# Reordering an eight-core hybrid decoder step on Trainium2: two tiles interleaved at the start, one output step moved, one factor kept in PSUM, later down-projections

## The chip, the cores and the metric

The kernel runs on all 8 NeuronCores of one Trainium2 chip, two dies of four cores (0 to 3 and 4 to 7). Every core works on its own sequence and its own 16 running tokens, so the cores don't exchange data, but they share the chip's memory. The metric is the device time in microseconds (us) of the slowest core. A few executions of any of these kernels fall in a slower state: some cores show a lower granted TensorE clock and the time is several per cent longer. All comparisons below are between fast executions.

## The reference, cut to what matters

One layer of a decoder trunk with 1024 channels: two token mixers in parallel (a causal pooling one and a gated short convolution), merged by sigmoid gates, then a gated feed-forward part with a short convolution. RMS norms stand before and after both parts.

```python
def trunk_layer(x, ...):
    h = rmsnorm(x, g_pre_mix)
    z = h @ w_in                                   # 1024 -> 4096
    u, v, bg, cg, ga, gb = jnp.split(z, IN_SPLITS, axis=-1)
    a, new_pool = multiscale_pool(u, buf_pool, pos0, w_pool, pool_scale)
    cv, new_conv = causal_dwconv(cg * v, buf_conv, w_conv)
    b = (bg * cv) @ w_conv_out
    merged = jax.nn.sigmoid(ga) * a + jax.nn.sigmoid(gb) * b
    x = x + rmsnorm(merged @ w_o, g_post_mix)
    h = rmsnorm(x, g_pre_ffn)
    upc, new_ffn = causal_dwconv(h @ w_up, buf_ffn, w_ffn_conv)    # 1024 -> 5632
    gate, val = jnp.split(upc, 2, axis=-1)
    y = (jax.nn.silu(gate) * val) @ w_down                         # 2816 -> 1024
    x = x + rmsnorm(y, g_post_ffn)
    return x, new_pool, new_conv, new_ffn
```

## The kernel before

Channels lie on the partitions and tokens along the free axis. One core's columns are cut into five mixing tiles (tile 0 of 512 columns, tiles 1 to 4 of 392) and then into six feed-forward (FFN) tiles of 344. The parts of a mixing tile, as the text calls them:

- **first half**: 16 blocks of the input projection (`F_block`), 8 matmuls each, with convolution and pooling on VectorE (DVE);
- **gates and merges** (`B`): 16 more blocks of the input projection for the gates, and 8 merges, which need the weights `w_pool` and `w_co`;
- **output step** (`WO`): 64 matmuls with `w_o`; ScalarE (ACT) evacuates each block into the buffer `R` and its square into `XSQ2`;
- **epilogue** (`epi`): the RMS factor, x added by an accumulating DMA, the result written to HBM by a DMA on the SyncE (SP) queue ("y write", in two halves), the second norm, and `h2` written to HBM for the FFN.

An RMS sum over the channels is made by DVE (`tree`, which adds 8 squares down to 2) and then two matmuls with a matrix of ones (`sums`), which go to a PSUM bank of their own. The other seven banks go round.

```python
def sums(rows, n, lo=0):
    pe([(bank(SB, n, lo), ONES, buf.ap[:, j, lo:n]) for buf, k, m in rows ...],
       ..., [("ps", SB)], n - lo, flt=True)        # flt: may float to another place in PE's order

def ln_exp(i, n, sq=None, lo=0):                   # rstd = exp(-0.5 * ln(mean + eps))
    s = SD.ap[:, i, lo:n]                          # in SBUF
    act(... out=s, in_=bank(SB, n, lo), func=AF.Ln ...)
    ...
    act(... out=s, in_=s, func=AF.Exp, scale=-0.5 ...)

def wo_evac(t, b, m):
    act(... out=R[t].ap[:, m, lo:N], in_=bank(b, N, lo), scale=cc(C_G2 + m) ...)       # L722
    act(... out=XSQ2[t].ap[:, m, lo:N], in_=bank(b, N, lo), func=AF.Square ...)        # L724

def epi_r(t, q):
    ...                                            # R *= rstd; R += x
    if q % 2:
        sp_dma(yT[:, ...], R[t].ap[...], [R[t].t(4 * h, 4)], [("y", t, h)], ...)       # the y write

def epi_x(t, k):
    if last:                                       # tile 4: scales R in place, so it needs the y write done
        act(... out=r, in_=r, scale=cc(C_G3 + k) ..., [..., ("y", t, k // 4)], ...)    # L776
        ...

def epi_y(t):                                      # end of an FFN tile
    sums([(YSQ, 0, 2)] ..., NB)
    ln_exp(0, NB)
    ...
    for q in range(4):                             # Y *= rstd, L868
        dve(... out=Y.ap[:, 2*q:2*q+2, :], in0=Y..., in1=SD.ap[:, 0, 0:NB]..., op=ALU.mult ...)
        pool_dma(yT[...], Y.ap[...], ..., acc=True)
```

A small scheduler in Python puts all operations into one order for each engine. PE's matmuls keep the order of the program, but the floating `sums` may go in where its model of time says that they are ready. Its rule for that is the line of the diff that begins with `if c is None or ready`, with `FLT` = 2500 ns. The cost model only decides the order; nothing in this document takes a time from it.

```python
    B(0)
    for t in range(1, NTA):                        # NTA = 5
        for i in range(16):
            F_block(t, i)
            if t == L: wup(1)                      # L = 4; one up-projection weight block is loaded
        if t < L:
            load_x(t + 1, 2, after=[wo[7]])
            ...
            prenorm(t + 1)
            WO(t - 1)
            epi(t - 1)
        ...
        B(t)                                       # for t == 4 with wup(2) after each merge
        if t == L - 1:
            WO(t, split=True)                      # tile 3's output step
            epi(t)
    WO(L, split=True, hook=lambda: wup(1))
    load_h2(0)                                     # the first FFN tile's input
```

`R` is one piece of memory for tiles 1 to 4. The weights of `w_in`, `w_co`, `w_up` and `w_dn` are read as f32 and cast to bf16 by DMAs on GpSimd's queue.

## Time and profile before

| | before |
|---|---|
| median of 3 runs | 844.45 us (842.34 to 845.41) |
| span of the slowest core in the profile (core 4) | 843.8 us |
| PE busy | 804.4 us |
| matmul work at full rate (5108 matmuls) | 792.0 us |

The last figure is an estimate. The Trainium skill, "TensorE: Matmul & The Clock Gate", Part 1 ("Wait — 56ns, not 53.3ns?"), gives N / 2.4 GHz + about 2.5 ns between the starts of warm back-to-back matmuls of N columns. The trace agrees: the median distances between the starts of two matmuls are 166 ns at 392 columns (the rule gives 165.8), 147 at 346 (146.7) and 216 at 512 (215.8). So what a matmul's distance to the next exceeds this rule is called *lost time* below. It contains waits and also matmuls at half the clock.

The page of the profile of the kernel before: busy time of the engines, and then PE's busy share and its granted clock in 40 equal slices of the span, in tenths.

```profile
PE 804.4 (95%) x5108; PEld 498.3 (59%) x5108; DVE 567.6 (67%) x1039; ACT 475.6 (56%) x924; POOL 261.5 (31%) x292
...
PE   6988899999999899999999999999999999999993
...
PEclk9997999999999999999999999999999999999997
```

TensorE is the bound: it is busy in nearly every slice, and no other engine comes over 67%. Only gaps can be won. They lie mainly in the first five slices, in slice 14 and in the last one. The windows view of core 4 before resolves four stretches. The columns are the window, its length, then busy us and instructions of PE, of PE's weight loads, of DVE, of ACT and of POOL, the granted clock, the DMA share and GB/s.

```profile
60.00:80.00 20.00, 14.93 (x55) 5.82 (x53) 6.30 (x10) 5.83 (x9) 5.00 (x7) 0.74 1.13 184
80.00:100.00 20.00, 17.50 (x82) 8.35 (x81) 12.77 (x21) 10.21 (x14) 0.00 (x0) 0.91 0.69 103
280.00:300.00 20.00, 17.71 (x98) 9.81 (x97) 10.56 (x19) 12.06 (x22) 1.46 (x2) 0.91 0.27 89
...
380.00:400.00 20.00, 20.00 (x138) 13.34 (x137) 18.60 (x37) 14.45 (x30) 19.95 (x18) 1.00 1.14 153
```

From 60 to 80 us PE ran 55 matmuls of 498 columns (210 ns each at full rate), or about 11.6 us of work; it shows as 14.93 us busy because part of them ran at half the clock. The waits view of PE in the kernel before says what it stood for (total us, times, the longest):

```profile
PE ps L463 <- DMA big<-w_co: 4.2, 2, 2.8
PE ps L463 <- ACT big L843: 3.4, 3, 1.2
...
PE ps L463 <- DMA big<-w_in: 3.2, 3, 2.3
...
PE ps L463 <- DVE big L544: 2.5, 1, 2.5
PE ps L463 <- ACT big L722: 2.3, 1, 2.3
```

`w_co` and `w_in` are the gate and merge weights of tile 0, which PE reaches before they have landed. L544 is tile 1's normalization. L722 is the evacuation of tile 3's output step; L843 is the evacuation of down-projections into `Y`. The timeline of core 4 before around 291 us shows what held L722 (start us, us, engine, line, operation, count, and in brackets the idle time before it and what ended it):

```profile
291.36 4.39 DVE L781 SCALAR_TENSOR_TENSOR big<-big 128x392 bf16<-128x392 f32 x8 [7.10 <-ACT big L724]
292.08 4.41 ACT L722 ACTIVATE big<-ps,big 128x392 f32<-128x392 f32 x8
...
292.81 5.49 PE L463 MATMUL ps<-big 128*128 128x392 bf16 x22 [2.29 <-ACT big L722]
```

DVE's L781 is the last step of tile 2's epilogue, which reads `R`; tile 3's evacuation follows it, and PE follows that, since its banks are full. The line view of the two multiplies by the RMS factor in the FFN of the kernel before (duration min/median/max in ns, first and last start in us, form):

```profile
L868 DVE TENSOR_TENSOR big<-big x20: 858/866/3450, 496.6 to 815.3; 128x688 f32<-128x688 f32 x20
```

```profile
L860 DVE TENSOR_TENSOR big<-big x4: 868/1588/2303, 832.2 to 836.0; 128x688 f32<-128x688 f32 x4
```

One of these multiplies takes 866 ns in the median and up to four times that.

### The profile page before, as it was taken

The page shows a single profiled execution, that of the slowest core. Times are in us where ns is not written, and L with a number is a line of the kernel's source. Part 1 is how long each engine was busy: PE and PEld are TensorE (multiplying, and loading weights), DVE is VectorE, ACT ScalarE, POOL GpSimd, SP SyncE. Part 2 cuts the span into 40 slices and gives each one's busy share as a digit, 9 for nine tenths or more (in the row PEclk, how much of TensorE's full clock was granted, in tenths as well). Part 3 has the DMA queues.
Part 4 walks back from the last instruction along what each step waited for, and adds up shares of the span by engine and source line. Part 5 has one row for each costly group of instructions (what it writes and reads, how often), then busy time and mean ns, then how long its engine had stood idle before and what let it go on. Part 6 is the DMA issues. An engine that isn't in the chain of part 4 may idle for free.

```text
span 843.8 us, 16663 instructions; the slowest of 8 cores (834.1 to 843.8 us)
## 1 busy us (share of the span) xinstructions
PE 804.4 (95%) x5108; PEld 498.3 (59%) x5108; DVE 567.6 (67%) x1039; ACT 475.6 (56%) x924; POOL 261.5 (31%) x292
## 2 busy tenths in 40 slices
PE   6988899999999899999999999999999999999993
PEld 4433455555555555566566666666666666666662
DVE  2753765787786587589776576568666865877723
ACT  3232569567656635787755555556555545665632
POOL 4532000201001063479582243224222422342222
PEclk9997999999999999999999999999999999999997
DMA  8999602813523499999990041014001500030062
GB/s 161 164 190 170 152 12 66 206 52 97 131 74 45 120 156 222 173 174 156 211 174 3 3 75 27 26 34 69 35 2 34 69 1 2 11 59 2 2 136 85
DMA packets 63206, 75.51 MB, mean 89 GB/s; under 512 B 2928, under 2 KB 59376, under 8 KB 63104
## 3 DMA queue, kind: packets, MB, share of 16 engines
q0 software_dynamic: 40720, 43.01, 35.6%
q1 hardware_dynamic: 22400, 31.45, 12.0%
q8 instruction: 43, 0.70, 0.3%
q14 instruction: 43, 0.35, 0.1%
HBM read 81.89 MB, written 22.90 MB: 124 GB/s over the span
## 4 chain that ended last, share of the span: by engine, by line
PE 84%; DMA 8%; issue 2%; DVE 2%; ACT 2%; POOL 1%; DVEq 0%; SPq 0%; ACTq 0%; POOLq 0%
PE ps L463 84%; DMA big<-w_co 4%; DMA big<-w_in 2%; DMA yT<-big 1%; DMA big<-xT 1%; POOL big L476 1%; DVE big L819 1%; ACT big L815 1%; DVE big L860 0%; ACT big L517 0%; DVE big L868 0%; ACT L517 0%; POOL big L755 0%; DVE big L544 0%; POOL big L833 0%
## 5 line engine op out<-in xcount | busy, mean ns | idle before, releaser
L463 PE MATMUL ps<-big 128*128 128x346 bf16 (+5 forms) x5108 | 804.4, 321 | 26.5 <-ACT big L532 4.8
L463 PEld LDWEIGHTS ps<-big 128*128 128x128 bf16 x5108 | 498.3, 99 | 332.2 <-issue 42.7
L819 DVE SCALAR_TENSOR_TENSOR big<-ps,big 128x344 f32<-128x344 f32 (+1 forms) x528 | 283.8, 570 | 95.9 <-ACT big L815 75.4
L833 POOL TENSOR_TENSOR big<-big 128x344 bf16<-128x344 f32 x132 | 125.6, 953 | 240.1 <-DVE big L819 172.0
L815 ACT ACTIVATE big<-ps,big 128x344 f32<-128x344 f32 (+1 forms) x264 | 140.0, 540 | 65.2 <-PE ps L463 61.5
L832 ACT ACTIVATE big<-big 128x344 f32<-128x344 f32 x132 | 64.1, 489 | 53.2 <-DVE big L819 50.8
L474 POOL DMA_DIRECT2D big<-xT x16 | 17.7, 1118 | 186.3 <-DVE big L705 108.4
L692 ACT ACTIVATE big<-ps 128x392 f32<-128x392 f32 (+1 forms) x80 | 38.9, 513 | 53.5 <-PE ps L463 28.5
L705 DVE SCALAR_TENSOR_TENSOR big<-ps,big 128x392 f32<-128x392 f32 (+1 forms) x40 | 25.8, 646 | 45.5 <-PE ps L463 41.4
L476 POOL DMA_DIRECT2D big<-w_up x36 | 29.1, 883 | 59.7 <-PE ps L463 52.3
L843 ACT ACTIVATE big<-ps,big 128x344 f32<-128x344 f32 x48 | 25.7, 546 | 36.4 <-PE ps L463 36.3
L507 DVE TENSOR_TENSOR big<-big 128x1568 bf16<-128x1568 bf16 (+3 forms) x28 | 22.7, 812 | 19.7 <-ACT big L724 19.1
L474 POOL DMA_DIRECT2D yT<-big x20 | 25.9, 1470 | 30.4 <-DVE big L819 16.0
L846 ACT ACTIVATE big<-ps 128x344 bf16<-128x344 f32 x48 | 21.7, 451 | 21.7 <-PE ps L463 18.3
L849 DVE TENSOR_TENSOR big<-big 128x688 bf16<-128x688 bf16 x17 | 8.8, 517 | 36.3 <-ACT big L846 36.3
L601 DVE TENSOR_TENSOR big<-big 128x406 f32<-128x406 f32 (+7 forms) x50 | 30.0, 600 | 3.6 <-ACT big L623 0.7
L868 DVE TENSOR_TENSOR big<-big 128x688 f32<-128x688 f32 x20 | 25.0, 1276 | 9.1 <-ACT big L522 9.1
L570 ACT ACTIVATE big<-big 128x392 f32<-128x392 f32 (+1 forms) x20 | 12.8, 639 | 31.7 <-DVE big L656 31.7
L722 ACT ACTIVATE big<-ps,big 128x392 f32<-128x392 f32 (+1 forms) x40 | 24.0, 608 | 10.2 <-PE ps L463 7.6
L476 POOL DMA_DIRECT2D big<-w_in x32 | 23.2, 745 | 19.9 <-DMA big<-xT 9.2
L573 DVE SCALAR_TENSOR_TENSOR big<-big 128x392 f32<-128x392 f32 (+1 forms) x40 | 25.6, 644 | 4.5 <-ACT big L570 3.8
L709 DVE TENSOR_TENSOR big<-ps,big 128x392 f32<-128x392 f32 (+1 forms) x40 | 23.4, 585 | 6.5 <-PE ps L463 5.7
(58 smaller groups left out, 379.9 us busy)
## 6 DMA issues: line engine op xcount, KB each, us to landing
big<-w_in POOLq DMA_DIRECT2D x32, 256.0 KB, 21.1
big<-w_up POOLq DMA_DIRECT2D x28, 256.0 KB, 21.0
yT<-big POOLq DMA_DIRECT2D x20, 344.0 KB, 5.5
yT<-big SPq DMA_DIRECT2D x8, 784.0 KB, 8.9
big<-w_dn POOLq DMA_DIRECT2D x8, 704.0 KB, 35.5
big<-xT SPq DMA_DIRECT2D x6, 784.0 KB, 4.8
big<-xT POOLq DMA_DIRECT2D x12, 392.0 KB, 7.2
big<-h2T SPq DMA_DIRECT2D x6, 692.0 KB, 4.6
```

The source lines that it names most:

```text
L463: ins = e.matmul(o, lhsT=l, rhs=x, start=(start and i == 0), stop=(stop and i == last))
L474: return S.add("pool", lambda e: e.dma_start(out=out, in_=in_, accum_op=ALU.add, max_dma_last_dim=mx), r, w, dma=True, byts=byts, pri=pri, ...
L476: return S.add("pool", lambda e: e.dma_start(out=out, in_=in_, max_dma_last_dim=mx), r, w, dma=True, byts=byts, pri=pri, after=after)
L573: dve(lambda e, k=k: e.scalar_tensor_tensor(out=cv, in0=p[:, 2 + k + lo:2 + k + N], scalar=cc(C_WC + 4 * k + c), in1=cv, op0=ALU.mult, op1 ...
L601: dve(lambda e, nx=nx, cur=cur, s=s, a2=a2: e.tensor_tensor(out=nx[:, a2:W], in0=cur[:, a2:W], in1=cur[:, a2 - s:W - s], op=ALU.add), [ct] ...
L692: act(lambda e, b=b, g=g: e.activation(out=GT[t].ap[:, g, lo:N], in_=bank(b, N, lo), func=AF.Sigmoid), [("ps", b)], [GT[t].t(g, 1)], N, ps ...
L705: dve(lambda e: e.scalar_tensor_tensor(out=A_, in0=bank(bp, N, lo), scalar=cc(C_PS + m), in1=A_, op0=ALU.mult, op1=ALU.mult), [("ps", bp), ...
L815: act(lambda e, b=b, fj=fj, tt=tt: e.activation(out=tt[:, 0:n], in_=bank(b, n), func=AF.Copy, scale=cc(C_WF + fj)), [("ps", b), KCST], [to ...
L819: dve(lambda e, b=b, fj=fj, tt=tt, k=k: e.scalar_tensor_tensor(out=tt[:, 0:n], in0=ps[:, b * 512 + k:b * 512 + k + n], scalar=cc(C_WF + 44 ...
L832: act(lambda e: e.activation(out=g, in_=g, func=AF.Silu), [T.t(0, 1)], [T.t(0, 1)], NB, tab="silu")
L833: S.add("pool", lambda e: e.tensor_tensor(out=gb.ap[:, j, :], in0=g, in1=v, op=ALU.mult), [T.t()], [gb.t(j, 1)], dur=NB * 2.17 + 100)
L843: act(lambda e: e.activation(out=Y.ap[:, m, :], in_=bank(b, NB), func=AF.Copy, scale=cc(C_G4 + m)), [("ps", b), KCST], [Y.t(m, 1)], NB, ps ...
```

## The change

Four things are moved, and no matmul is added or removed:

1. The first half of tile 1 is interleaved with the last blocks of tile 0's first half and goes before tile 0's gates and merges; tile 0's output step follows its merges. The gate weights get more time to land. Tile 1's x is loaded by GpSimd's queue between the weights, and the first weight loads wait for one quarter of tile 0's x instead of two. Buffers are laid out anew for it.
2. Tile 3's output step and epilogue move from before tile 4's first half to after seven of its blocks.
3. The FFN's RMS factor is kept in PSUM, so that the multiply has one SBUF input instead of two; and the eight down-projections of an FFN tile start at the sixth pair of up-projections instead of the third.
4. The rule for the floating sums is eased: a sum that the program needs soon may go in when it is modelled to be ready 400 ns ahead, instead of 2500 ns.

```diff
-                        if c is None or ready[f.idx] + FLT <= s or sf <= s - 200.0:
+                        if c is None or ready[f.idx] + (FLT if f.pri > s + 8000.0 else 400.0) <= s or sf <= s - 200.0:
...
-    X = per_tile(KC, False, [o_x] * NTA)
-    R = per_tile(KC, False, [o_r] + [X[1].end] * 4)
+    X = per_tile(KC, False, [o_x, W_O.off] + [o_x] * 3)
+    R = per_tile(KC, False, [o_r] + [X[2].end] * 4)
...   (other buffers of tile 1 moved in the same way)
-    def ln_exp(i, n, sq=None, lo=0):
+    def ln_exp(i, n, sq=None, lo=0, ps_out=False):
         s = SD.ap[:, i, lo:n]
+        out, tok = (bank(SB, n, lo), ("ps", SB)) if ps_out else (s, SD.t(i, 1))
...
-        ln_exp(0, NB)
+        ln_exp(0, NB, ps_out=True)
+        sdb = bank(SB, NB).unsqueeze(1).to_broadcast([128, 2, NB])
...   (both multiplies of epi_y read sdb)
-    wd += [wload(W_IN, w_in, i, 1, BL, after=[xs0[1]]) for i in range(1, 16)]
+    wd += [wload(W_IN, w_in, i, 1, BL, after=[xs0[0]]) for i in range(1, 16)]
...
+    for q in range(4):
+        pool_dma(X[1].flat[...], xT[1][...], ..., after=[xs0[1]], pri=-1e6)
...
-    for i in range(NRAW, 16):
+    prenorm(1)
+    wo = [wload(W_O, w_o, m, 1, BL, after=[xs0[1]]) for m in range(8)]
+    for i in range(NRAW, 12):
         F_block(0, i)
-    load_x(1, 4, after=[wd[20]])
-    prenorm(1)
+    for i in range(4):
+        F_block(1, i)
+        F_block(0, 12 + i)
+    for i in range(4, 16):
+        F_block(1, i)
...
     B(0)
+    load_x(2, 2, after=[wo[7]])
+    prenorm(2)
+    WO(0, split=True)
+    epi(0)
+    B(1)
+    load_states()
+    for t in range(2, L):
...   (as before for tiles 2 and 3)
+    for i in range(16):
+        F_block(L, i)
+        wup(1)
+        if i == 6:
+            WO(L - 1)
+            epi(L - 1)
+    small_states()
+    B(L)
...
-    WD = {2: 0, 5: 1, 8: 2, 10: 3, 13: 4, 15: 5, 18: 6, 21: 7}
+    WD = {5: 0, 7: 1, 10: 2, 12: 3, 14: 4, 16: 5, 19: 6, 21: 7}
```

A line of the kernel after has a number one higher than the same line before, from the end of `sums` on (L868 before is L869 after, L722 is L723).

## The prediction

> **What bounds the kernel now.** TensorE. The page shows it busy 804 of 843.8 us, and 84% of the chain that ended last is its matmuls. In the table of 20 us stretches PE is at 20.00 nearly everywhere, DVE at 11 to 19. So only PE's gaps can be won. From start-to-start distances of matmuls in the trace (slowest core; yardstick: about 123 matmuls of 392 columns in a steady 20 us) I estimate 792 us of matmul work and 36 us lost between first and last matmul:
> - 0 to 40 us: 8.5 us (x and first weights arrive).
> - 40 to 95 us: 15 us (other cores 7.5 to 14). Tile 0's gates and merges wait for weights: the waits view has PE <- DMA w_co 4.2 and w_in 3.2 us; the stretch 60:80 has PE busy 14.9 us at clock 0.74; 2.5 us are a wait for tile 1's normalization (L544). The Trainium skill, "TensorE: Matmul & The Clock Gate" (HAM oscillation), says idle gaps over about 3.4 us halve the clock[...].
> - 287 us: 4.1 us, ACT's evacuation of tile 3's output step (L722) waiting for DVE L781: tiles 2 and 3 share R.
> - 500, 580, 660 us: 1.3 us each, at the third pair of a tile. DVE's Y*rstd multiplies (L868) have a median of 866 ns but a maximum of 3450 ns.
> - the rest: about 4 us in 400-415 and at the last down-projections.
>
> **The change.** No matmul is added or removed.
> 1. Tile 1's first half (128 matmuls, 21 us) moves ahead of tile 0's merges and needs only weights already there. Gate weights then have until about 69 us instead of 46; they land by about 69 before, with the same bytes. The waits of 40-95 go: -14 us. Cost: tile 1's x (1.6 MB; its load took about 10 us beside the weights) cuts in after about four weight blocks and delays later ones by about 5 us; as weights start about 3 us earlier, I charge +2 us. DVE has about 50 us of work in 20-70 us; pooling can be put off into the merges.
> 2. Tile 3's output step after seven blocks of tile 4: epilogue 2 has long read R: -4 us.
> 3. rstd in PSUM: the multiply then has one SBUF input. The Trainium skill, "SBUF — State Buffer" (Who interferes with whom), says two SBUF inputs contend with a GpSimd op that reads SBUF, one doesn't; L868's 866 to 3450 ns agrees. I expect all near 870 ns. With the first down-projection three pairs later, the 1.3 us stalls go: -4 us; the tail (L860, 6.1 us for four) wins 0.5 to 1.
> 4. Earlier float-in of the sums, and tile 0's output step straight after its merges: perhaps +1 us.
>
> Sum: about -20 us, nearly all on the critical path. Predicted 824.5 us, range 817 to 833. Chances: faster by over 2% 0.70, within 2% 0.29, slower 0.01.
>
> **Would show it right.** PE at 20.00 and clock 1.00 in all stretches from 40 to 100 us; no PE <- DMA w_co; no stall near 270-290; L868 maximum under 1000 ns; PE <- ACT L843 gone.
>
> **Would make it wrong.** Weight blocks after x1 over 5 us late, so the loss moves to 25-40 us; DVE too full in 40-70 us, so evacuation holds the PSUM banks; sums floated in before their squares are ready; tile 3's epilogue colliding with up-projection loads; six pairs without down-projection overfilling DVE.

## The result, and the profile after

| | before | after |
|---|---|---|
| median | 844.93 us (842.34 to 846.17, 4 runs) | 832.31 us (831.09 to 832.64, 4 runs) |
| ratio of fast runs | | 0.9852, 95% interval 0.9826 to 0.9878 |
| span of the slowest core in the profile | 843.8 us | 830.5 us (core 5) |
| mean span of the 8 cores in the profile | 840.0 us | 827.8 us |

A ratio here is the mean time of one kernel's fast runs over that of the other's of the same rounds, so it is not quite the ratio of the medians. All runs were correct. The change gains 12.6 us, or 1.5%; it is faster, but by less than the 2% which the prediction thought most likely.

The lost time by phase, in us, as the mean of the eight cores (worked out from the starts of all matmuls in the traces; a gap counts where it begins; the first FFN tile runs from 3 us before the first up-projection to 62 us after it, and the last down-projections begin after the last up-projection, about 31.5 us before the last matmul):

| | to 40 us | 40 to 100 us | 100 us to FFN | first FFN tile | rest of FFN | last down-projections | after the last matmul | sum |
|---|---|---|---|---|---|---|---|---|
| before | 8.1 | 12.4 | 4.2 | 1.4 | 4.2 | 1.7 | 13.4 | 45.4 |
| after | 11.4 | 0.1 | 0.0 | 7.8 | 0.3 | 2.0 | 11.6 | 33.3 |
| gain | -3.3 | +12.3 | +4.2 | -6.4 | +3.8 | -0.3 | +1.8 | +12.1 |

The sum of gains, 12.1 us, accounts for the drop of the mean span (840.0 to 827.8 us). The new loss is in the first FFN tile. The windows view of core 5 after, with the columns as before:

```profile
20.00:40.00 20.00, 17.46 (x76) 7.62 (x75) 16.25 (x27) 7.78 (x14) 8.93 (x13) 0.91 1.12 203
...
60.00:80.00 20.00, 20.00 (x110) 10.66 (x109) 15.28 (x29) 7.62 (x18) 6.24 (x9) 1.00 1.15 159
80.00:100.00 20.00, 20.00 (x97) 9.33 (x96) 8.70 (x13) 5.49 (x10) 0.00 (x0) 1.00 0.82 171
280.00:300.00 20.00, 20.00 (x123) 11.81 (x121) 13.50 (x30) 11.18 (x22) 4.96 (x7) 1.00 0.92 135
340.00:360.00 20.00, 17.57 (x119) 11.20 (x117) 9.68 (x18) 13.45 (x25) 7.40 (x10) 1.00 1.09 156
380.00:400.00 20.00, 16.75 (x115) 10.97 (x113) 17.47 (x33) 15.26 (x31) 16.35 (x16) 1.00 1.15 200
```

The stretches 60 to 100 and 280 to 300 us are full now, at clock 1.00. A new gap stands at 20 to 40 us, and two more at 340 to 360 and 380 to 400, where the kernel before had 20.00 (at 380). The waits of PE in the kernel after (core 5):

```profile
PE ps L463 <- DVE big L507: 4.2, 2, 3.3
...
PE ps L463 <- DMA big<-w_in: 2.5, 1, 2.5
PE ps L463 <- ACT big L725: 1.5, 1, 1.5
PE ps L463 <- DVE big L820: 1.3, 2, 1.0
```

The waits for `w_co`, L843, L544 and L722 are gone. L507 is new at this size: it is `tree`, DVE's step before a floating sum. L725 is tile 4's evacuation. The timeline of core 5 after shows both new stalls:

```profile
344.92 0.59 ACT L723 ACTIVATE big<-ps,big 128x392 f32<-128x392 f32 x1 [7.11 <-DMA yT<-big]
...
346.04 3.68 PE L463 MATMUL ps<-big 128*128 128x346 bf16 x24 [1.47 <-ACT big L725]
...
395.47 0.62 ACT L777 ACTIVATE big<-big 128x392 f32<-128x392 f32 x1 [2.66 <-DMA yT<-big]
...
399.44 4.81 PE L463 MATMUL ps<-big 128*128 128x392 bf16 x20 [3.25 <-DVE big L507]
```

First, ACT waits 7.11 us for a DMA of `yT` before it may write `R`, and PE then stands behind ACT's evacuation. Second, at about 396 us ACT again waits for a DMA of `yT` (tile 4's own, before the in-place scaling); PE then stands 3.25 us at a floating sum for `tree`. Whether the wait of ACT makes `tree` late, or the sum has been put too early, these lines don't tell; E7 settles it. The multiplies by the RMS factor in the kernel after:

```profile
L869 DVE TENSOR_TENSOR big<-big,ps x20: 858/862/872, 488.7 to 800.1; 128x688 f32<-128x688 f32 x20
```

```profile
L861 DVE TENSOR_TENSOR big<-big,ps x4: 862/864/870, 820.3 to 822.6; 128x688 f32<-128x688 f32 x4
```

Their scatter is gone: the longest is 872 ns instead of 3450.

### The profile page after: what moved, and what is told of

It reads as the page before. It is cut to its first block, busy times and chain, and to the rows that moved or that the text cites. A ratio compares the mean times of both kernels' runs of the same rounds, so it can differ in the third digit from the quotient of the medians.

```text
span 830.5 us, 16670 instructions; the slowest of 8 cores (820.3 to 830.5 us)
## 1 busy us (share of the span) xinstructions
PE 801.2 (96%) x5108; PEld 499.5 (60%) x5108; DVE 555.9 (67%) x1039; ACT 475.4 (57%) x923; POOL 262.7 (32%) x296
## 4 chain that ended last, share of the span: by engine, by line
PE 83%; DMA 8%; issue 2%; POOL 2%; ACT 2%; DVE 1%; DVEq 0%; ACTq 0%; POOLq 0%; SPq 0%
PE ps L463 83%; DMA yT<-big 4%; DMA big<-w_in 2%; DMA big<-xT 2%; POOL big L476 1%; DVE big L820 1%; ACT big L816 1%; POOL big L834 1%; POOL big L676 0%; ACT L833 0%; DVE big L861 0%; DVEq L1031 0%; ACT big L833 0%; POOL big L756 0%; ACT big L723 0%
## 5 line engine op out<-in xcount | busy, mean ns | idle before, releaser
L463 PE MATMUL ps<-big 128*128 128x346 bf16 (+6 forms) x5108 | 801.2, 320 | 17.8 <-DVE big L507 4.2
L474 POOL DMA_DIRECT2D big<-xT x16 | 15.6, 1015 | 178.4 <-DVE big L706 107.8
L844 ACT ACTIVATE big<-ps,big 128x344 f32<-128x344 f32 x48 | 26.0, 548 | 54.2 <-PE ps L463 52.9
L507 DVE TENSOR_TENSOR big<-big 128x1568 bf16<-128x1568 bf16 (+3 forms) x28 | 22.8, 818 | 31.7 <-ACT big L725 31.0
L723 ACT ACTIVATE big<-ps,big 128x392 f32<-128x392 f32 (+1 forms) x40 | 24.6, 614 | 18.9 <-PE ps L463 10.9
L847 ACT ACTIVATE big<-ps 128x344 bf16<-128x344 f32 x48 | 21.7, 452 | 15.6 <-PE ps L463 13.1
L712 DVE TENSOR_TENSOR big<-big 128x392 bf16<-128x392 f32 (+1 forms) x40 | 23.1, 586 | 2.4
L545 DVE SCALAR_TENSOR_TENSOR big<-big 128x392 bf16<-128x392 f32 (+1 forms) x40 | 24.2, 645 | 0.1
```

Of the source, the lines that this page charges most:

```text
L463: ins = e.matmul(o, lhsT=l, rhs=x, start=(start and i == 0), stop=(stop and i == last))
L474: return S.add("pool", lambda e: e.dma_start(out=out, in_=in_, accum_op=ALU.add, max_dma_last_dim=mx), r, w, dma=True, byts=byts, pri=pri, ...
L844: act(lambda e: e.activation(out=Y.ap[:, m, :], in_=bank(b, NB), func=AF.Copy, scale=cc(C_G4 + m)), [("ps", b), KCST], [Y.t(m, 1)], NB, ps ...
```

## The experiments

The kernels of one batch ran on one chip with runs of the kernel before between them. Batch 1 (chip 4): E1 to E4. Batch 2 (chip 13): C1, E6, E7, E8. Batch 3 (chip 0): E5, E11. Batch 4 (chip 3): E14, E13. The kernel before took 850.31, 847.48, 845.29 and 850.66 us in the four (medians of its fast runs; one run of batch 2, at 884.86 us, was slow), so a kernel is compared inside its batch, or by its ratio to the kernel before. All gave the correct result. The lost time of each (mean of cores, as above; for the fast profiles only):

| | to 40 us | 40 to 100 | 100 to FFN | first FFN tile | rest of FFN | last downs | tail | median us (fast runs) | ratio to before (95%) |
|---|---|---|---|---|---|---|---|---|---|
| C1, after again | 11.6 | 0.1 | 0.0 | 7.9 | 0.5 | 2.0 | 11.5 | 834.11 | 0.9842 (0.9827, 0.9857) |
| E1, old sum rule | 12.2 | 1.3 | 0.4 | 5.6 | 0.6 | 1.7 | 11.5 | 832.91 | 0.9805 (0.9775, 0.9835) |
| E2, tile 3's step back | 12.0 | 0.2 | 2.1 | 8.7 | 1.4 | 1.7 | 11.5 | 838.42 | 0.9858 (0.9839, 0.9877) |
| E3, rstd in SBUF | 12.1 | 0.1 | 0.0 | 10.2 | 1.9 | 2.0 | 13.4 | 838.89 | 0.9874 (0.9844, 0.9903) |
| E4, early downs | 12.0 | 0.1 | 0.0 | 10.0 | 1.9 | 2.0 | 11.6 | 837.15 | 0.9845 (0.9827, 0.9863) |
| E5, interleave only | 11.4 | 1.3 | 4.0 | 3.2 | 3.7 | 2.0 | 13.4 | 838.07, 839.21 | none (2 fast runs) |
| E7, old rule in tile 4 | 11.7 | 0.1 | 0.0 | 3.7 | 0.5 | 2.0 | 11.5 | 829.55 | 0.9787 (0.9771, 0.9803) |
| E8, three loads moved | 12.5 | 7.7 | 0.0 | 2.6 | 6.3 | 1.8 | 11.5 | 842.85 | 0.9943 (0.9926, 0.9959) |
| E11, early state | 11.3 | 0.1 | 0.0 | 3.5 | 0.7 | 2.0 | 11.7 | 827.83 | 0.9786 (0.9768, 0.9805) |
| E14, step after block 4 | 12.8 | 0.1 | 0.1 | 4.5 | 0.7 | 1.7 | 11.7 | 829.48 | 0.9756 (0.9730, 0.9783) |
| E13, and late downs | 12.3 | 0.1 | 0.2 | 4.4 | 0.7 | 1.7 | 11.5 | 828.72 | 0.9749 (0.9727, 0.9772) |

Two theories were set against each other at first for the new loss in the first FFN tile. Theory A: the moved output step of tile 3 makes its y write late, and tile 4's evacuation waits for it. Theory B: the new sum rule puts the sums of tile 4's epilogue too early.

### E1: the old rule for the floating sums everywhere

```diff
-ready[f.idx] + (FLT if f.pri > s + 8000.0 else 400.0) <= s
+ready[f.idx] + FLT <= s
```

> The changed kernel with one thing undone: the sums are floated in by the old rule (2500 ns of margin always, not 400 when urgent). Question: where do the 9 us come from that TensorE loses between 340 and 400 us in the changed kernel (2.5 us at the same place before)? Theory A: moving tile 3's output step into tile 4's first half put its y write (24.9 us to landing) beside the up-projection loads; tile 4's output step reuses R and waits for it, and the backlog costs the 4 us at 340-370; the new sum rule has no part in that. Theory B: the new rule puts the sums one pair too early, so that TensorE waits for the tree (L507). A alone predicts this run at 340-370 unchanged (3 to 4 us lost) and the same total within 1 us. B predicts that the losses at 350 (1 us) and 391 (3.3 to 4.7 us) fall, and the total by 3 to 5 us. I expect a split: 391 falls to 1 to 2.5 us, 340-346 stays; total 829 to 831.

Measured: 832.91 us and a ratio of 0.9805. In the same batch the nearest thing to the unchanged kernel is E4 at 837.15 us, so the old rule is worth about 4 us on that chip. The first FFN tile loses 5.6 us instead of 10.0, and the rest of the FFN 0.6 instead of 1.9. In return 1.2 us come back at 40 to 100 us: there the new rule is right. So theory B holds for a large part, but the old rule everywhere isn't the answer either.

### E2: tile 3's output step back in its old place

```diff
+    WO(L - 1, split=True)
+    epi(L - 1)
     for i in range(16):
         F_block(L, i)
         wup(1)
-        if i == 6:
-            WO(L - 1)
-            epi(L - 1)
```

> The changed kernel with tile 3's output step and epilogue back where they were, after tile 3's merges. Theory A (the moved step makes the y write late and tile 4's output step wait for it): the loss at 340-370 falls from about 4 us to under 1 us, the wait of L723 for the y write (7.1 us) goes, and the stall of 4.1 us near 275 comes back; total within 1 us of the changed kernel. Theory B (sum rule): 340-370 keeps its loss, the 4.1 us come on top, total 835 to 837.

Measured: 838.42 us, 0.9858. A part of the stall before the FFN comes back: 2.1 us, where 4.1 were expected. The first FFN tile still loses 8.7 us, against 10.0 in E4: theory A, as first put, falls. The trace says why: the second half of the y write left only at 21.7 us before the FFN's start on most cores, still after the load of the first FFN tile's input, and landed between 5.8 us before and 3.6 us after that start. It left 0.1 to 0.3 us after the last DMA that adds x into `R` had landed, on every core: it waited for its data. Moving the step back didn't put the write back.

### E3: the RMS factor in SBUF again

```diff
-        ln_exp(0, NB, ps_out=True)
-        sdb = bank(SB, NB).unsqueeze(1).to_broadcast([128, 2, NB])
+        ln_exp(0, NB)
+        sdb = SD.ap[:, 0, 0:NB].unsqueeze(1).to_broadcast([128, 2, NB])
```

> The changed kernel with the FFN rstd back in SBUF (the down-projections stay late). Theory P (the second SBUF input of the multiply is what collides with GpSimd): the multiply's maximum returns to over 2.5 us, and near 490, 570 and 650 us TensorE loses 1 to 1.3 us each, total +3 to +4 us. Theory W (the later first down-projection is what took the stalls away): the multiply's maximum returns, but TensorE loses nothing there; total +0 to +0.5 us, with up to 1 us from the tail.

Measured: 838.89 us, 0.9874; 1.7 us slower than E4, which differs from the kernel after in the down-projections alone. The multiplies of E3:

```profile
L869 DVE TENSOR_TENSOR big<-big x20: 857/866/1591, 494.3 to 805.7; 128x688 f32<-128x688 f32 x20
```

```profile
L861 DVE TENSOR_TENSOR big<-big x4: 869/1588/2304, 825.9 to 829.7; 128x688 f32<-128x688 f32 x4
```

The four multiplies at the end scatter again as in the kernel before, and the tail is 13.4 us instead of 11.6. That is all of PSUM's own gain: 1.8 us. The three stalls of the FFN do not come back here, with the down-projections still late. The multiplies of the FFN come back only to 1591 ns, on no core over 2.5 us as expected, so the later down-projections also take away a part of the scatter.

### E4: the down-projections early again

```diff
-    WD = {5: 0, 7: 1, 10: 2, 12: 3, 14: 4, 16: 5, 19: 6, 21: 7}
+    WD = {2: 0, 5: 1, 8: 2, 10: 3, 13: 4, 15: 5, 18: 6, 21: 7}
```

> The changed kernel with the old places of the down-projections (first after the third pair); rstd stays in PSUM. Theory P: no multiply over 1.0 us, no stall near 490, 570 and 650 us, total unchanged within 0.5 us. Theory W: the multiply stays short, but three stalls of about 1.3 us return, total +4 us.

Measured: 837.15 us, 0.9845, where C1 has 0.9842 on another chip. No stall comes back in the FFN, and L869 has a maximum of 871 ns. With the factor in PSUM the later down-projections add nothing that these runs resolve.

### C1: the kernel after once more

No edit.

> The changed kernel itself, as control on the same chip as the next three, because the chip of the first four runs had a slower time for the kernel before (850 instead of 845 us). Expected ratio 0.980 to 0.986; TensorE loses 7 to 10 us in the first tile of the FFN on most cores, about 0 between 40 and 340 us.

Measured: 834.11 us, 0.9842, first FFN tile 7.9 us. The result repeats in another batch, on chip 13.

### E6: fewer weight loads while the y write is under way

```diff
     for i in range(16):
         F_block(L, i)
-        wup(1)
+        if i <= 6:
+            wup(1)
...
             if t == NTA - 1:
-                wup(2)
+                wup(3)
```

> The changed kernel with the up-projection loads held back in the second half of tile 4's first half (seven loads, then three at each of tile 4's merges), so that tile 3's x adds and y write meet less traffic. Moving the step back did not take the loss away, so theory A in its first form fell. Theory C: what makes tile 4's output step wait is tile 3's y write landing late, and what makes it late is the queue of weight loads in front of the x adds and beside the write. C predicts: the write lands by 335 us, L723 does not wait for it, TensorE's losses of 1.4 and 1.1 us near 341 and 346 us and the backlog stall near 366 us go; first FFN tile 3 to 4 us better, total 2 to 4 us better than the control. Rival D: the first FFN tile is simply too full on ScalarE (four table loads in ten us) and stalls with or without the late write; then under 1 us is won.

Measured: five of the six runs were slow; the one fast run took 837.94 us, against 834.11 for C1. There is no ratio, and the profile is one of a slow run in which cores 2 to 7 stayed at a clock of 0.98 to 0.99. I use it only for the order of things on cores 4 to 7. There both halves of the y write left before the FFN's input load (about 35 and 25 us before the FFN's start) and landed about 24 and 13 us before it, so tile 4's evacuation didn't wait. But the input itself landed 0.3 us before the start on each of them, PE waited for it and for up-projection weights (2.1 and 2.8 us on core 4), and these cores lost 9.9 to 11.4 us in the first FFN tile. The load was moved, not taken away. As a measure of the y write the experiment is inconclusive.

### E7: the old rule for the two sums of tile 4's epilogue only

```diff
-ready[f.idx] + (FLT if f.pri > s + 8000.0 else 400.0) <= s
+ready[f.idx] + (FLT if f.late or f.pri > s + 8000.0 else 400.0) <= s
...   (late is set by rstd() in epi_n1 and epi_n2 for tile 4)
```

> The changed kernel with the old rule for the sums of tile 4's epilogue alone; all other sums keep the new rule. Theory B (sum floated in one pair too early): the stall near 391 us falls from 3.5 to 4.7 us to about 2, and the 1.2 us at 40 us and 0.8 us near 787 us that the run with the old rule everywhere lost do not come; total 2 to 3 us better than the control. If the run equals the control, the stall at 391 is the y write's wait alone and the place of the sums has no part in it.

Measured: 829.55 us, 0.9787. It is 4.6 us faster than C1 in the same rounds, and the intervals of the two ratios don't touch. The order of PE's instructions differs in one place: the second pair of sums stands 312 up-projection matmuls behind the first pair, as in the kernel before, and not 296. One pair of up-projections, 16 matmuls, is all that it needed. The 0.8 us near 787 us that the expectation names are no loss of the old rule: 0.8 to 1.1 us are lost there under both rules. The first FFN tile loses 3.7 us instead of 7.9. The wait of PE for `tree` between 380 and 410 us, in C1 and then in E7 (core 5 of both):

```profile
PE ps L463 <- DVE big L507: 5.4, 1, 5.4
```

```profile
PE ps L463 <- DVE big L508: 0.3, 1, 0.3
```

The waits of PE in E7 (core 1) from 330 to 410 us:

```profile
PE ps L463 <- DVE big L821: 3.6, 3, 2.3
PE ps L463 <- DVE big L508: 1.1, 2, 1.0
```

L508 is `tree`, and its 1.0 us here belongs to the first pair of sums. After 380 us it now costs PE at most 0.3 us on any core, where C1 had 2.3 to 5.4 us on its eight cores. There is a second part to the gain. In C1 seven of eight cores run 8 to 18 matmuls in that tile at twice the normal distance, that is at half the clock, which costs 1.45 us in the mean of all cores; in E7 only one core does (0.16 us in the mean). Such a stall is paid twice, except on core 4 of C1, where after 2.3 us no matmul ran at half the clock.

What is left in E7 goes with the other wait. Per core, ACT's wait for the y write at L724, and the loss in the first FFN tile, in us, in order of the wait:

| core | 6 | 4 | 2 | 7 | 3 | 0 | 1 | 5 |
|---|---|---|---|---|---|---|---|---|
| wait of ACT for yT | 0 | 2.6 | 3.6 | 4.4 | 4.8 | 5.3 | 5.5 | 6.7 |
| loss of PE | 0.5 | 1.4 | 2.1 | 3.5 | 4.4 | 5.2 | 7.0 | 5.7 |

The core whose y write lands in time loses next to nothing.

### E8: E6 and E7 together, with two more loads moved

```diff
   (E6 and E7, and:)
-                if j in (3, 5, 8, 10, 13, 15, 18, 20):
+                if j in (3, 5, 8, 10):
                     wdn()
+            if t == 1 and j in (0, 1, 3, 5):
+                wdn()                      # half of w_down a tile later
...
-    wd += [wload(W_IN, w_in, i, 1, BL, after=[xs0[0]]) for i in range(1, 16)]
+    wd += [wload(W_IN, w_in, i, 1, BL, after=[xs0[0]], pri=-2e6 if i < 9 else 0) for i in range(1, 16)]
                                            # tile 1's x three weight blocks later
```

> Attempt at a better kernel: up-projection loads held back, old rule for the sums of tile 4's epilogue, four of the eight down-projection loads moved into the second FFN tile (so that tile 4's y write meets less traffic), and tile 1's x loaded after nine instead of six weight blocks. If the causes are as read: first FFN tile loses under 2.5 us instead of 8, start 1.5 to 2.5 us less, total 7 to 9 us better than the control. If the down-projection weights then come late, a wait for them appears after 400 us.

Measured: 842.85 us in the median of three fast runs (a fourth, at 863.63 us, was slow), 0.9943, so it gives nearly all of the gain back. The two longest waits of PE in E8 (core 1):

```profile
PE ps L463 <- DVE big L546: 4.9, 1, 4.9
PE ps L463 <- ACT big L845: 4.7, 1, 4.7
```

L546 is tile 1's normalization, from 44 us on: with x three blocks later, tile 1 isn't ready when PE gets there. To have x in early was right. The start, which was to lose 1.5 to 2.5 us less, lost 12.5 us against 11.6 in C1. L845, for which PE stood from 439 to 444 us, is the evacuation of a down-projection into `Y`. Two things held it: `Y` shares its memory with the FFN's carried state, which GpSimd read until 439.9 us, and ScalarE itself stood 7.3 us at L848 for a DMA of `h2T`, until 439.3 us; which of them decides isn't shown. The first FFN tile itself lost 2.6 us, the least of all the runs with the change.

### E5: only the interleave

All of E1, E2, E3 and E4 together, so that of the change only its first part is left.

> The interleaving of tiles 0 and 1 alone: old rule for the sums, tile 3's step back after its merges, rstd in SBUF, early down-projections. Three questions. 1: What is the interleaving worth by itself? From the control, 12.4 us of waits in 40-100 us go and 3 us come at the start: total -8 to -10 us against the kernel before. 2: The three stalls of 1.3 us in the FFN: each remedy alone kept them away, so with both undone they must come back (near 490, 570, 650 us) if they are what the two remedies cure; if they stay away, neither was needed. 3: First FFN tile: 1 to 2.5 us lost, as before the change, if the new loss comes from the sum rule and the moved step; 3 to 5 us if it comes with the interleaving itself.

Measured: two fast runs at 838.07 and 839.21 us, and two slow ones, so there is no ratio. The kernel before had 845.29 on this chip; the interleave alone is worth about 6 to 7 us net, where 8 to 10 were expected. The lost time has all the old stalls: 4.0 us before the FFN, 13.4 us in the tail, and three waits in the FFN for the evacuation L844 (2.5 us together on core 7), which neither E3 nor E4 had. Each of the two remedies for those stalls is enough by itself. And the interleave costs 3.3 us at the start here too (11.4 against 8.1).

It also shows the order of the SyncE queue. The timelines of SP in three kernels, near the same place. Kernel before, core 4:

```profile
322.47 6.93 SPq L470 DMA_DIRECT2D yT<-big  x2
333.59 0.54 SPq L470 DMA_DIRECT2D big<-h2T  x1
```

Kernel after, core 5:

```profile
315.86 0.38 SPq L470 DMA_DIRECT2D yT<-big  x1
318.25 0.54 SPq L470 DMA_DIRECT2D big<-h2T  x1
319.85 1.81 SPq L470 DMA_DIRECT2D yT<-big  x1
```

E5, core 7:

```profile
311.14 10.31 SPq L470 DMA_DIRECT2D yT<-big  x2
322.88 0.54 SPq L470 DMA_DIRECT2D big<-h2T  x1
```

Before and in E5 both halves of tile 3's y write leave ahead of the load of the FFN's input (`h2T`). In the kernel after the second half leaves behind it, and it leaves when its data are there: on all eight cores within 0.2 us of the landing of the last DMA that adds x into `R`, which is 0.5 to 2.8 us after the input load has left. Counted from issue to landing, that half takes 10 to 13 us before (it lands 18.0 to 11.2 us before the FFN's start on the eight cores) and 20 to 25 us after (it lands from 1.7 us before the start to 4.6 us after it). In E5 no core waits at tile 4's evacuation for it. Yet E5 loses 3.2 us in the first FFN tile, where the kernel before lost 1.4; on core 7, 2.2 us of it are a wait for the FFN's input. So an early write doesn't come free either.

### E11: E7, and the FFN's carried state loaded early

```diff
   (E7, and:)
-    ST_FFN = Buf(Y.off, 44, 2 * NS)
+    ST_FFN = Buf(h2b.off, 44, 2 * NS)
...
         B(t)
+        if t == 2:
+            pre_ffn()
...   (pre_ffn() no longer in FFN tile 1; tile 4's in-place scaling a little later in ACT's order)
```

> A second attempt at a better kernel, from the one with the old rule for tile 4's sums (ratio 0.9787): the FFN state of the decoded tokens is loaded and multiplied in the third tile of the first half instead of at the start of the second FFN tile, and tile 4's in-place scaling on ScalarE (which waits for the y write and holds up all of ScalarE behind it) is put later in ScalarE's order. If the stall near 392 us (2.3 us) is that wait at the head of ScalarE's queue, it falls under 1 us, and 427 to 434 us (0.4 us) goes; total 2 to 3 us better than the kernel with the old rule for tile 4's sums, ratio about 0.975. If the y write holds something else too (the tree, h2), it only moves.

Measured: 827.83 us, fast runs 826.77 to 828.62, and 0.9786; two of six runs were slow. The first FFN tile loses 3.5 us and the rest of the FFN 0.7. E7 on another chip has 0.9787, so nothing is resolved between the two.

### E14: E11, with tile 3's output step after four blocks instead of seven

```diff
-        if i == 6:
+        if i == 3:
             WO(L - 1)
             epi(L - 1)
```

> The kernel with early FFN state and the old rule for tile 4's sums (ratio 0.9786), with tile 3's output step after four instead of seven blocks of tile 4. Theory: what is left of the loss in the first FFN tile is the wait of tile 4's evacuation (L723 of the changed kernel) for tile 3's y write, whose longest landing is 20 to 25 us on every core where the step was moved and 11 to 13 us where it was not, and core by core the loss grows with that wait (2 to 3 us of wait: 0.5 to 1.4 us lost; over 4: 3 to 7). Four us earlier, the wait should fall by 3 to 4 us, the first FFN tile's mean loss from 3.5 to 1.5 us or less, the total by 2 to 3 us (ratio about 0.976). If the stall near 275 us comes back in part, the step is now too early for epilogue 2.

Measured: 829.48 us, 0.9756. This is over 2% faster than the kernel before with its whole interval. The ratio is the expected one, but by luck: the purpose was missed, with 4.5 us lost in the first FFN tile where 1.5 or less were expected. The timeline of SP in E14, core 3:

```profile
311.12 0.38 SPq L471 DMA_DIRECT2D yT<-big  x1
320.45 0.54 SPq L471 DMA_DIRECT2D big<-h2T  x1
321.19 0.90 SPq L471 DMA_DIRECT2D yT<-big  x1
```

The first half of the y write leaves 6 us earlier than in the kernel after, counted from the FFN's start, but the second half leaves 0.7 us behind the input load, at 21.8 us before the start on all eight cores, and lands 1.1 to 3.5 us after it. On seven of eight cores it is held by its place in SP's order: its last x add landed 0.7 to 2.5 us earlier (on core 7, 0.1 us). To start four blocks in, instead of seven, isn't early enough to get ahead of that place.

### E13: E14, with half of the down-projection weights a tile later

```diff
   (E14, and the w_dn part of E8)
```

> The same with four of the eight down-projection loads moved into the second FFN tile. If tile 4's y write is slow because of these loads, the wait of the in-place scaling for it (2 to 5 us) goes and another 1 us is won against the run before; if the loads come late for their use, stalls appear from 410 us on.

Measured: 828.72 us, 0.9749, with the first FFN tile at 4.4 us. E14, in the same rounds, isn't distinguishable from it. Later weights neither help nor, with the state early, hurt.

By their ratios, E7, E11, E14 and E13 beat both the kernel before and the kernel after; E7 was also run beside the latter. E7 is the smallest edit. Which of the four is best isn't settled: they ran on three chips, and by lost time E7 and E11 (sum 29.5 and 29.3) look a little better than E14 and E13 (31.6 and 30.8).

## Why the prediction was right or wrong

The predicted time was 824.5 us with a range of 817 to 833; the kernel took 832.31 us. That is within the range, at its upper edge, and the class held most likely (faster by over 2%, 0.70) didn't come. The sum promised 20 us and 12.6 came. That the time still fell inside the range is partly luck: the prediction has no term for the 6.4 us lost in the first FFN tile, and they happened to be less than the 8.5 us between 824.5 and 833. All five signs that were to show it right came true on the slowest core; none of them watched the place to which the loss moved. Point by point:

- **"Tile 1's first half moves ahead of tile 0's merges ... the waits of 40-95 go: -14 us."** Right. The loss from 40 to 100 us fell by 12.3 us, to 0.1, on the mean of the cores. On the slowest core of each profile it fell from 15.1 to 0.0. The granted clock of 60 to 80 us went from 0.74 to 1.00 with the gaps. Of the kernel before's loss there, 2.6 us in the mean were matmuls at half the clock. The prediction tied the 0.74 to idle gaps over about 3.4 us; on core 4 the longest wait of PE there was 2.81 us.
- **"I charge +2 us."** Too low. The start costs 3.3 us more. Of it, 2.2 us in the mean fall between 26 and 40 us, where PE waits for a `w_in` block behind tile 1's x (1.7 us in the mean, 2.54 on core 5). This was named as a risk. The other 1.1 us, earlier, have no cause shown. E8 showed that it is still the better side: with x later, PE loses 7.7 us at 40 to 100, and the start isn't faster.
- **"Tile 3's output step ... -4 us."** Right about the stall: 4.2 us to 0.0, and E5 has it back with 4.0. What that move took with it, the y write, was missed; see below.
- **"With the first down-projection three pairs later, the 1.3 us stalls go: -4 us."** Right: they go, and the rest of the FFN gained 3.8 us. The credit was shared out wrongly: E3 and E4 show that either remedy alone is enough, and E5 that without both the stalls are there.
- **"The tail wins 0.5 to 1."** It won 1.8 us, all by PSUM (E3). The Trainium skill, "SBUF — State Buffer" (Who interferes with whom), states that a DVE instruction with two SBUF inputs contends with a GpSimd instruction that reads SBUF, and one with at most one SBUF input doesn't. The trace agrees: 858 to 3450 ns with two, 858 to 872 ns with one. Over the eight cores before, 40 of the 160 multiplies of L868 took over 1000 ns, and each of these overlapped a GpSimd tensor instruction; none without such an overlap took over 876 ns. After, 96 overlap one and the longest takes 872 ns. The page gives no size for the contention. The four multiplies took 6.1 us from the first start to the last end before and take 3.2 us with one input in PSUM; 1.8 of these 2.9 us reach the end of the kernel, and the prediction had counted on at most 1.
- **"Earlier float-in of the sums ... perhaps +1 us."** This is the step that failed; the sum took it as a cost of 1 us, and it was mis-sized. The new rule wins 1.2 us at 40 to 100 us (E1 against the kernel after); the last down-projections lose 1.7 to 2.0 us under both rules. But it puts tile 4's second sums one pair too early, and PE stands at them. That alone costs 4.1 us of lost time and 4.6 us of measured time (C1 against E7): a wait of 2.3 to 5.4 us on every core, and on most cores some ten matmuls at half the clock after it. The prediction had named "sums floated in before their squares are ready" as a risk, but hadn't worked out where the rule would bite.
- **Not predicted at all: the y write behind the FFN's input load.** I read `R` as shared between tiles 2 and 3, which the moved step relieves, and didn't read on that tiles 3 and 4 share it too, and that tile 3's y write would now have its second half behind the input load on SP's queue, because its data come too late to leave ahead. The Trainium skill, "DMA: Bandwidth & Descriptors" (Queues, rings and completion order), states that on each DMA engine descriptors are consumed in ring order, and that an engine takes turns between the queue rows that have work. The packet records of core 5 after agree with both. The second half leaves 21.0 us before the FFN's start, but its first packet (1568 bytes) starts at 6.1 us before, when the input load's packets (692 bytes, from 16.5 to 4.5 us before) run out. In the ten us from 16 to 6 us before, SP's queue moved about 660 KB and GpSimd's, with the casting loads of `w_up`, about 940 KB. So the write takes 10 to 13 us ahead of that load, and 20 to 25 us behind it. ACT then waits for up to 8.5 us (C1, core 0).

How the missing 6.4 us of the first FFN tile divide: 4.1 us are the sums, which E7 isolates. The remaining 2.3 us (E7's 3.7 less the 1.4 of before) go with the wait for the y write across the cores of E7; that is a correlation, since no run took this wait away without a new one. E5 and E6 put the write ahead of the input load and lost time to the input, and E14 missed its aim. A version that puts the second half ahead of the input load in SP's order and leaves everything else as in E7 wasn't run, so what it would gain stays open. It would hold the input load back: in E7 the last x add lands 0.9 to 2.8 us after that load has left. Also open is why E5 loses 1.8 us more there than the kernel before with the same order of the writes; the input lands later (0.2 to 3.9 us before the start against 0.2 to 5.5), which explains a part on some cores.

## What to carry to other kernels

When an operation moves earlier or later, follow its outgoing DMAs as well as its inputs: ask which buffer they still hold, when their own data arrive, and what they will now stand behind on their queue. An eased scheduling rule should be checked at every place where it bites, because a wait of 3 us on the engine that bounds the kernel can cost a further 1 to 2.6 us in half-rate matmuls after it (C1). Where two remedies for one stall come together, undo each alone before crediting both.

## What the Trainium skill lacked or had wrong

- "TensorE: Matmul & The Clock Gate" (HAM oscillation) puts the idle gap after which the clock halves at more than about 3.4 us. Here shorter gaps were enough: in the kernel after, core 5, a wait of 2.54 us at 28 us was followed, from 31.85 us on, by 500-column matmuls 415 to 419 ns apart (500 / 1.2 GHz is 416.7), and in the kernel before a wait of 2.29 us at 290 us by about ten matmuls at half rate (1.6 us of loss). In the stretch of the kernel before that had 0.74 the longest wait was 2.81 us. Not every such gap does it: in C1, core 4, a wait of 2.3 us at 389 us had no half-rate matmul after it.
- The same page (Part 1, the peak-current limiter) tells one to budget 1.95 GHz for sustained dense matmul on all cores. In fast runs all eight cores were granted 0.98 to 0.99 of full speed with PE busy 95% of the time, and matmuls at the full 2.4 GHz distance; mean clocks of 0.81 to 0.86 (cores of 929 to 988 us) and of 0.92 to 0.96 (859 to 887 us) showed only in slow executions. The one profile of a slow execution (E6) has the page's third state, 13/16, for 162.8 us, but on cores 0 and 1 alone: cores 2 and 3 of the same die never left the other two states, where the page has the whole die change.
- "SBUF — State Buffer" (Who interferes with whom) has the rule for the shared port but no size. Here a 128x688 f32 multiply took 866 ns in the median and up to 3450 ns with two SBUF inputs, at most 872 ns with one in PSUM; for the kernel's tail that was 1.8 us.
- "DMA: Bandwidth & Descriptors" fits one DMA alone, issued from GpSimd, as 2.0 us + bytes / 436e3; by that fit one half of a y write (784 KB) would take an estimated 3.8 us, though it is issued by SP, for which the page has no fit. It has no figure for several busy queues. Here the same write took 10 to 13 us ahead of another load on its queue and 20 to 25 us behind it, with casting weight loads running on GpSimd's queue.
